# Doubling triangular inverses: all products of a step in front of its copies

## The chip, the cores and the metric

The kernel runs on one core of one Trainium2 chip. The metric is the device time of one execution in microseconds (us), median of several runs. TensorE (PE) multiplies and writes to PSUM; VectorE (DVE) and ScalarE (ACT) read PSUM and work in SBUF; GpSimd (POOL) works in SBUF; SyncE (SP) issues most DMA. Each engine takes its instructions in one fixed order and waits on semaphores for what others make.

## The reference

Two layers on 256 tokens of width 1024. Each layer adds half a SwiGLU feed-forward block (inner width 2816), a mixer, and half a feed-forward block again; all matrices are float32. The mixer projects the normed input with `w_in`, gives one part to a bidirectional gated DeltaNet (4 heads of 128) and one to a Hyena group (512 channels), and maps both back with `w_out`:

```python
o_dn = _deltanet_group(q, k, v, z, beta_logit, alpha, ...)
o_hy = _hyena_group(hy_in, hy_conv[i], ...)
x = x + jnp.concatenate([o_dn, o_hy], axis=-1) @ w_out[i]
```

The DeltaNet works in chunks and needs, for each head, chunk and direction, the solution of a unit triangular system:

```python
a_mat = jnp.where(strict, jnp.einsum("bhnid,bhnjd->bhnij", kb, k) * decay, 0.0)
a_mat = a_mat + jnp.eye(c, dtype=q.dtype)
sol = lax.linalg.triangular_solve(a_mat, rhs, left_side=True, lower=True, unit_diagonal=True)
```

The output of each head is normed (`_rmsnorm(o, norm_w)`) and multiplied by `silu(z)`; the Hyena output is normed too.

## The kernel before

The kernel uses chunks of 128 tokens, so there are 2 chunks x 2 directions x 4 heads = 16 systems of 128x128. They stand in four quads `q_` = 0 to 3 of four heads each: quads 0 and 1 are the forward direction (first and second chunk), quads 2 and 3 the backward one (`S[:, 8 + h]` and `S[:, 12 + h]`). Two tiles hold the inverses as they grow: `S`, and `ST`, its transpose. Blocks of 16 are made first, and the stage "lvl" joins them to 32 (tiles `pz`, `pp`). The stage "quad" doubles twice, n = 32 and n = 64: for each pair of blocks a, b one product `pzq` (off-diagonal block of the system by `ST`), a copy to SBUF by ScalarE (`zq`), and then a product each for `S` (copied with a sign by VectorE) and `ST` (copied by ScalarE), both in one PSUM tile `ppq`. At n = 64 quads 0 and 1 need only `S`, quads 2 and 3 only `ST`.

Products of n = 32 occupy a 32x32 part of TensorE's array, those of n = 64 a 64x64 part, all others the whole 128x128.

Around it stand, by stage: "lc1" (long convolution of Hyena: `py`, `ze`, `zo`), "z" (projection `pw` of the gate z), "hn" (products `py2`, the Hyena norm: sums `st`, `nv`, GpSimd's power `pw__3775`, `dg`, `rbp`, `rb`), "hw" (`yn`, split in a high and a low half `yp` by ScalarE and VectorE, then the products `acc` of the Hyena half of `w_out`), "solve" (eight groups `ph` with VectorE and ScalarE steps `uf`, `ub`, `rho`, `gv` between), "o" (`po`; squares `osq`, sums `oss`, GpSimd's powers `pw__3991` and `pw__4013`, `on`), "ow" (transposes `pot`, gate `og`, split `yp`, and the DeltaNet half of `acc`). The names with numbers are those of layer 1; layer 2 has the same with others.

The program is written in this sequence, but it isn't executed in it: a scheduler of the framework simulates the engines and orders the instructions of each by readiness and by priorities of the stages (table `PRM`, `stage(...)`). So a change of dependences in "quad" lays out everything around it anew. VectorE also makes the low halves of the weights (`wl`), after ScalarE's high halves (`wh`); GpSimd makes the low halves of weights for the next block (`early`). All matrix products but `pot` go through one helper and show as line 118.

PSUM is taken by tags with two buffers each: `pzq`, `ph` and `po` have tag a, `pot` tag b, `py` tag c, `ppq` tag d, and the accumulators `acc` take c and d.

Of the kernel before, what the change touches and what calls it, by code (L numbers as in the profile page):

```python
# [10 lines left out]
F32 = mybir.dt.float32  # L11
# [78 lines left out]
def trunk_kernel(ctx: ExitStack, tc: tile.TileContext, xt, ffn, wba, win, wout, par, fpar, fwo, fnorm, con, feat, wnd, out):  # L90
# [7 lines left out]
    mx = ctx.enter_context(tc.tile_pool(name="mx", bufs=1))  # L98
# [15 lines left out]
    def psum(tag, name, shape=(128, 4, 128)):  # L114
        return ps.tile(list(shape), F32, tag=tag, name=name, bufs=2)

    def mm(o, l, r, start=True, stop=True, **kw):
        PE.matmul(o, lhsT=l, rhs=r, start=start, stop=stop, **kw)  # L118
# [72 lines left out]
    def rsqrt(v, n, tag):  # L191

        if tag[:2] in PRM["powr"]:
            y = sm.tile([128, n], F32, tag=tag, name="pw_")
            G.tensor_tensor(out=y, in0=v, in1=mhalf[:, 0:n], op=ALU.pow)
            return y
        sh = sm.tile([128, n], U32, tag=f"ns{n}", name="ns")
        V.tensor_scalar(out=sh, in0=v.bitcast(U32), scalar1=1, scalar2=None, op0=ALU.logical_shift_right)
        y0 = sm.tile([128, n], I32, tag=f"ny{n}", name="ny")
        V.tensor_scalar(out=y0, in0=sh.bitcast(I32), scalar1=-1.0, scalar2=float(0x5f3759df), op0=ALU.mult, op1=ALU.add)  # L200
        y = y0.bitcast(F32)
        for i in range(3):
            a = sm.tile([128, n], F32, tag=f"na{n}", name="na")
            V.tensor_tensor(out=a, in0=y, in1=y, op=ALU.mult)
            b = sm.tile([128, n], F32, tag=f"nb{n}", name="nb")
            V.scalar_tensor_tensor(out=b, in0=a, scalar=-0.5, in1=v, op0=ALU.mult, op1=ALU.mult)
            c = sm.tile([128, n], F32, tag=tag if i == 2 else f"nc{n}", name="nc_")
            V.scalar_tensor_tensor(out=c, in0=b, scalar=1.5, in1=y, op0=ALU.add, op1=ALU.mult)
            y = c
        return y  # L210
# [296 lines left out]
    def mixer(l, ys, norm, ab, wcols):  # L507
# [202 lines left out]
        for a in range(2):  # L710
            for hp in (slice(0, 2), slice(2, 4)):
                p = psum("a", "gram", (128, 2, 2, 128))
                for i in range(2):
                    h = hp.start + i
                    mm(p[:, i], kq[:, h, 0, a * 128:(a + 1) * 128], kq[:, h, 0])
                for i in range(2):
                    h = hp.start + i
# [18 lines left out]
        for a in range(2):  # L736
            both, one = ((Ef0, Eb[0, 0]), (Eb1, Ef[1, 1]))[a]
            for hp in (slice(0, 2), slice(2, 4)):
                p = psum("d", "kqp", (128, 2, 2, 128))
                for i in range(2):  # L740
                    h = hp.start + i
# [30 lines left out]
        for r in range(6, -1, -1):  # L772
            n = 7 - r
# [21 lines left out]
        S = mx.tile([128, 16, 128], F32, tag="S", name="S", bufs=1)  # L795
# [22 lines left out]
        for q_ in range(4):  # L818
            qs = slice(4 * q_, 4 * q_ + 4)
            p = psum("a", "stp")  # L820
# [10 lines left out]
        for q_ in range(4):  # L831
# [8 lines left out]
            pp = psum("d", "pp", (128, 2, 4, 4, 16))  # L840
# [38 lines left out]
        stage("quad")  # L879

        for n in (32, 64):
            for q_ in range(4):
                qs = slice(4 * q_, 4 * q_ + 4)
                pz = psum("a", "pzq", (128, 4, n))
                pp = psum("d", "ppq", (128, 4, n))
                zq = mx.tile([128, 4, n], F32, tag=f"zq{n}", name="zq", bufs=(2 if n == 32 else 1))
                for o in range(0, 128, 2 * n):
                    a, b = slice(o, o + n), slice(o + n, o + 2 * n)
                    for h in range(4):
                        mm(pz[b, h], XX[q_][a, h, b], ST[a, 4 * q_ + h, a])  # L890
                    A.activation(out=zq[b], in_=pz[b], func=AF.Copy)
                    if n == 32 or q_ < 2:
                        for h in range(4):
                            mm(pp[a, h], zq[b, h], S[b, 4 * q_ + h, b])
                        V.tensor_scalar(out=S[a, qs, b], in0=pp[a], scalar1=-1.0, scalar2=None, op0=ALU.mult)
                    if n == 32 or q_ >= 2:
                        for h in range(4):
                            mm(pp[b, h], S[b, 4 * q_ + h, b], zq[b, h])
                        A.activation(out=ST[b, qs, a], in_=pp[b], func=AF.Copy, scale=-1.0)

        stage("lc1")
# [19 lines left out]
        for i in range(4):  # L921
            c = slice(i * 128, (i + 1) * 128)
# [24 lines left out]
        def heads(tag, lh, r):  # L947
            p = psum(tag, "ph")
            for h in range(4):
                mm(p[:, h], lh(h), r[:, h])  # L950
            return p
# [12 lines left out]
        p = heads("a", lambda h: ST[:, 12 + h], gv1)  # L964
        ub[1] = d2("ub1")
        A.activation(out=ub[1], in_=p, func=AF.Copy)
        p = heads("a", lambda h: Mf[:, h], uf[0])
        V.tensor_tensor(out=rho[1], in0=rho[1], in1=p, op=ALU.subtract)
        p = heads("a", lambda h: Mb[:, h], ub[1])
# [3 lines left out]
        p = heads("a", lambda h: ST[:, 8 + h], gv0)  # L973
# [6 lines left out]
        for i in range(2):  # L980
# [10 lines left out]
            f = rsqrt(ss, 4, f"of{i}")  # L991
# [34 lines left out]
    for l in range(DEPTH):  # L1026
        P = par_s[:, l]
        ab = []
        side = chain(filters(l, ab), repeat(0, PRM["ej"]), ahead([win[l, i] for i in range(8)], PRM["ea"]))
        ys, norm = ffn_block(l, 0, ys, norm, P[:, C_NM:C_NM + 8], side)  # L1030
        ys, norm = mixer(l, ys, norm, ab, P[:, C_N2:C_N2 + 8])
        nxt = par_s[:, l + 1, C_N1:C_N1 + 8] if l + 1 < DEPTH else None
        ws = [ffn[l + 1, 0, j, i] for j in range(2) for i in range(2)] if l + 1 < DEPTH else []
        ys, norm = ffn_block(l, 1, ys, norm, nxt, chain(repeat(0, PRM["fj"]), ahead(ws, PRM["fa"])))
# [114 lines left out]
```

## Time and profile before

| What | Value |
|---|---|
| median of 3 runs | 1250.51 us (1249.68 to 1251.75) |
| profiled execution | 1253.56 us, span 1251.8 us |
| mean granted clock of TensorE | 0.982 |
| busy share of the span | PE 97%, DVE 70%, ACT 47%, POOL 25% |
| chain that ended last | PE 71%, DVE 13%, DMA 8%, ACT 3%, issue 3%, POOL 1% |

The span is the time from the first to the last instruction; the execution's own time also holds what lies around it. The chain follows the work back from the last instruction, at each step to what released it. The granted clock tells how fast the chip let TensorE run: 1.0 is full speed, 0.5 half. Line numbers below are those of the kernel before; in the changed one lines behind the stage are five higher.

### The profile page before, as it was taken

The numbers are of one execution on the slowest core, as the hardware profiler recorded it, in microseconds if no ns is written. First come the engines' busy times: TensorE is split into PE (matmuls) and PEld (weight loads), VectorE is DVE, ScalarE is ACT, GpSimd is POOL, SyncE is SP. The second block draws the span as 40 slices with busy tenths as digits, with TensorE's granted clock in tenths as the row PEclk, the third lists the DMA queues.
The fourth block names the chain that finished last, engine by engine and source line by source line (L and its number), as shares of the span: only waits on it lengthen the run. The fifth ranks groups of instructions, "written<-read, shape, count | busy, mean of one in ns | idle before, by whom it ended". The sixth has DMA issues, their size and how long they took to land.

```text
span 1251.8 us, 20519 instructions
## 1 busy us (share of the span) xinstructions
PE 1210.9 (97%) x7908; PEld 1063.9 (85%) x7908; DVE 875.5 (70%) x1483; ACT 588.8 (47%) x1058; POOL 306.8 (25%) x254
## 2 busy tenths in 40 slices
PE   6999989999999999999999999999999999999997
PEld 5888878978779899998888888888887898999996
DVE  6866677659954666667777767776597656766665
ACT  5544455362323445555554445553432334555553
POOL 5122233211221521113221214430202314111111
PEclk9999999999998899999999999999999988999998
DMA  8555667123222445556645556650231414455551
GB/s 292 172 168 192 195 204 228 31 68 101 69 74 96 135 135 188 190 188 204 210 127 188 181 168 210 222 169 16 77 111 51 136 60 143 156 186 188 193 186 53
DMA packets 53913, 186.36 MB, mean 149 GB/s; under 512 B 6157, under 2 KB 7088, under 8 KB 53816
## 3 DMA queue, kind: packets, MB, share of 16 engines
q1 hardware_dynamic: 50156, 179.01, 43.9%
q10 hardware_dynamic: 3660, 6.05, 1.6%
q8 instruction: 62, 1.02, 0.3%
q14 instruction: 35, 0.29, 0.1%
HBM read 183.98 MB, written 1.05 MB: 148 GB/s over the span
## 4 chain that ended last, share of the span: by engine, by line
PE 71%; DVE 13%; DMA 8%; ACT 3%; issue 3%; POOL 1%; DVEq 0%; SPq 0%; ACTq 0%
PE acc L118 18%; PE g L118 15%; PE u L118 14%; PE pw L118 10%; DMA raw<-in_win 6%; DVE wl L182 4%; DMA raw<-in_ffn 2%; PE py L118 1%; ACT wh L179 1%; PE pe L118 1%; PE pp L118 1%; PE ppq L118 1%; PE ph L118 1%; PE st L118 1%; DVE vs L552 1%
## 5 line engine op out<-in xcount | busy, mean ns | idle before, releaser
L182 DVE TENSOR_TENSOR wl<-raw,wh 128x1024 fp32r<-128x1024 f32 (+1 forms) x270 | 341.4, 1267 | 84.8 <-ACT wh L179 81.2
L179 ACT ACTIVATE wh<-raw 128x1024 fp32r<-128x1024 f32 (+1 forms) x270 | 282.1, 1048 | 121.0 <-PE acc L118 76.0
L118 PE MATMUL acc<-hp,wh 128*128 128x256 f32 x1408 | 265.9, 282 | 0.0
L118 PE MATMUL g<-yp,wh 128*128 128x512 f32 x656 | 245.0, 407 | 8.6 <-DVE yp L157 8.6
L118 PE MATMUL u<-yp,wh 128*128 128x512 f32 x656 | 236.0, 395 | 0.5 <-DVE ub L333 0.3
L118 PEld LDWEIGHTS acc<-hp,wh 128*128 128x128 f32 x1408 | 227.4, 190 | 3.6 <-issue 0.8
L368 POOL TENSOR_TENSOR sr<-gb,rb 128x256 f32<-128x256 f32 x88 | 110.4, 1254 | 450.7 <-ACT gb L366 450.7
L118 PE MATMUL acc<-hp,wl 128*128 128x256 f32 x704 | 194.3, 284 | 8.7 <-DVE wl L182 8.7
L118 PE MATMUL u<-yp,wl 128*128 128x256 f32 x656 | 168.9, 278 | 2.9 <-DVE wl L182 2.9
L118 PE MATMUL g<-yp,wl 128*128 128x256 f32 x656 | 171.7, 282 | 0.0
L118 PEld LDWEIGHTS g<-yp,wh 128*128 128x128 f32 x656 | 124.2, 189 | 40.6 <-DVE yp L157 9.7
L118 PE MATMUL pw<-y,raw 128*128 128x256 f32 x640 | 148.6, 381 | 0.0
L118 PEld LDWEIGHTS acc<-hp,wl 128*128 128x128 f32 x704 | 133.3, 190 | 13.0 <-DVE wl L182 11.1
L118 PEld LDWEIGHTS u<-yp,wh 128*128 128x128 f32 x656 | 123.2, 188 | 22.6 <-PE g L118 0.6
L118 PEld LDWEIGHTS pw<-y,raw 128*128 128x128 f32 x640 | 120.1, 190 | 25.9 <-issue 11.5
L118 PEld LDWEIGHTS u<-yp,wl 128*128 128x128 f32 x656 | 122.9, 188 | 11.3 <-DVE wl L182 4.3
L118 PEld LDWEIGHTS g<-yp,wl 128*128 128x128 f32 x656 | 124.6, 191 | 5.2 <-issue 1.4
L182 POOL TENSOR_TENSOR early<-raw,early 128x512 fp32r<-128x512 f32 (+1 forms) x44 | 75.5, 1729 | 93.9 <-ACT early L179 93.9
L332 ACT ACTIVATE gb<-g 128x256 f32<-128x256 f32 x88 | 33.4, 380 | 120.7 <-PE g L118 117.7
L153 DVE TENSOR_TENSOR hp<-ub,hp 128x256 fp32r<-128x256 f32 x88 | 56.8, 645 | 26.8 <-ACT hp L152 26.6
L333 DVE TENSOR_TENSOR gb<-g,gb 128x256 f32<-128x256 f32 x88 | 37.0, 420 | 44.3 <-ACT gb L332 44.3
L333 DVE TENSOR_TENSOR ub<-u,ub 128x256 f32<-128x256 f32 x88 | 37.0, 420 | 38.4 <-ACT ub L332 38.4
(436 smaller groups left out, 1669.8 us busy)
## 6 DMA issues: line engine op xcount, KB each, us to landing
raw<-in_ffn SPq DMA_DIRECT2D x264, 512.0 KB, 3.9
raw<-in_win SPq DMA_DIRECT2D x56, 512.0 KB, 4.5
raw<-in_wout SPq DMA_DIRECT2D x16, 512.0 KB, 3.9
w<-in_wnd ACTq DMA_DIRECT2D x16, 256.0 KB, 4.4
wo<-in_fwo ACTq DMA_DIRECT2D x8, 130.0 KB
X<-in_xt SPq DMA_DIRECT2D x4, 256.0 KB, 7.5
con_s<-in_con SPq DMA_DIRECT2D x1, 544.0 KB, 9.2
out<-X SPq DMA_DIRECT2D x2, 256.0 KB, 2.5
```

The source lines that it names most:

```text
L118: PE.matmul(o, lhsT=l, rhs=r, start=start, stop=stop, **kw)
L153: eng.tensor_tensor(out=lo, in0=src, in1=hi.bitcast(F32), op=ALU.subtract)
L179: op = A.activation(out=h, in_=raw[:, c], func=AF.Copy)
L182: eng.tensor_tensor(out=l_, in0=raw[:, c], in1=h.bitcast(F32), op=ALU.subtract)
L332: A.activation(out=t, in_=o[:, 1], func=AF.Copy)
L333: V.tensor_tensor(out=t, in0=o[:, 0], in1=t, op=ALU.add)
L368: G.tensor_tensor(out=sr, in0=sg, in1=norm.rb, op=ALU.mult)
L552: i = V.scalar_tensor_tensor(out=dst[:, lo:hi], in0=raw[:, lo + s_:hi + s_], scalar=P[:, w0 + j:w0 + j + 1], in1=dst[:, lo:hi], op0=ALU.mu ...
```

## The change

Only the stage "quad" is rewritten. The quads come in the sequence 0, 3, 1, 2. Within a quad the `pzq` products of all pairs stand first, then their copies `zq`, then all products for `S` and `ST`, alternating per head, and then all copies. The SBUF tiles `zq` of both levels share two buffers (named `zqd`); before, n = 32 had two and n = 64 one. Since VectorE's and ScalarE's copies of a quad read the same PSUM tile `ppq` and now stand one behind the other, they wait for each other (`S` of the first pair, `ST` of the first, `S` of the second, ...).

```diff
@@ -879,23 +879,28 @@
         stage("quad")
 
         for n in (32, 64):
-            for q_ in range(4):
+            for q_ in (0, 3, 1, 2):
                 qs = slice(4 * q_, 4 * q_ + 4)
                 pz = psum("a", "pzq", (128, 4, n))
                 pp = psum("d", "ppq", (128, 4, n))
-                zq = mx.tile([128, 4, n], F32, tag=f"zq{n}", name="zq", bufs=(2 if n == 32 else 1))
-                for o in range(0, 128, 2 * n):
-                    a, b = slice(o, o + n), slice(o + n, o + 2 * n)
+                zq = mx.tile([128, 256], F32, tag="zq", name="zqd", bufs=2)[:, 0:4 * n].rearrange("p (h c) -> p h c", h=4)
+                halves = [(slice(o, o + n), slice(o + n, o + 2 * n)) for o in range(0, 128, 2 * n)]
+                to_s, to_st = n == 32 or q_ < 2, n == 32 or q_ >= 2
+                for a, b in halves:
                     for h in range(4):
                         mm(pz[b, h], XX[q_][a, h, b], ST[a, 4 * q_ + h, a])
+                for a, b in halves:
                     A.activation(out=zq[b], in_=pz[b], func=AF.Copy)
-                    if n == 32 or q_ < 2:
-                        for h in range(4):
+                for a, b in halves:
+                    for h in range(4):
+                        if to_s:
                             mm(pp[a, h], zq[b, h], S[b, 4 * q_ + h, b])
+                        if to_st:
+                            mm(pp[b, h], S[b, 4 * q_ + h, b], zq[b, h])
+                for a, b in halves:
+                    if to_s:
                         V.tensor_scalar(out=S[a, qs, b], in0=pp[a], scalar1=-1.0, scalar2=None, op0=ALU.mult)
-                    if n == 32 or q_ >= 2:
-                        for h in range(4):
-                            mm(pp[b, h], S[b, 4 * q_ + h, b], zq[b, h])
+                    if to_st:
                         A.activation(out=ST[b, qs, a], in_=pp[b], func=AF.Copy, scale=-1.0)
 
         stage("lc1")
```

The scheduler's order of the engines shows where this goes. TensorE, layer 1, the first 32-wide quads between the products of the z projection (`pw`) and of the convolution (`zo`, `ze`); before:

```order
L118 MATMUL pw<-y_2422,raw 128x256 x2
L118 MATMUL ppq<-S,zq 32x32 x4
L118 MATMUL pzq<-ST,ex 32x32 x3
L118 MATMUL ppq<-S,zq 32x32 x4
L118 MATMUL pzq<-ST,ex 32x32 x5
L118 MATMUL zo<-zt,con_s 128x512
L118 MATMUL pw<-y_2417,raw 128x256 x4
L118 MATMUL pw<-y_2422,raw 128x256 x4
L118 MATMUL ppq<-zq,S 32x32 x8
L118 MATMUL ze<-zt,con_s 128x512
L118 MATMUL pw<-y_2417,raw 128x256 x2
```

and after, from the end of the first group of sixteen `ppq` products on:

```order
L118 MATMUL ppq<-zqd,S 32x32
L118 MATMUL ppq<-S,zqd 32x32
L118 MATMUL ppq<-zqd,S 32x32
L118 MATMUL pzq<-ST,ex 32x32 x8
L118 MATMUL pzq<-ST,xf 32x32 x8
L118 MATMUL zo<-zt,con_s 128x512
L118 MATMUL pw<-y_2417,raw 128x256 x3
L118 MATMUL pw<-y_2422,raw 128x256 x4
L118 MATMUL pw<-y_2417,raw 128x256 x2
L118 MATMUL ppq<-S,zqd 32x32
L118 MATMUL ppq<-zqd,S 32x32
```

The products for S and ST of several quads, and the next `pzq`, are now in one run instead of four groups with `pw` between.

TensorE, layer 1, from the Hyena half of `acc` to the DeltaNet half, before:

```order
L118 MATMUL acc<-yp,wl 128x256
L118 MATMUL acc<-yp,wh 128x256 x2
L118 MATMUL acc<-yp,wl 128x256
L118 MATMUL acc<-yp,wh 128x256
L997 MATMUL pot<-con_s,on 128x128 x8
L118 MATMUL acc<-yp,wh 128x256
L118 MATMUL acc<-yp,wl 128x256
```

and after, where the end of `po` and the beginning of the Hyena half of `acc` meet:

```order
L118 MATMUL po<-uf_3964,ef_2510 128x128
L118 MATMUL po<-ub_3943,eb_2499 128x128
L118 MATMUL po<-uf_3936,ef_2498 128x128
L118 MATMUL po<-uf_3964,ef_2510 128x128
L118 MATMUL po<-ub_3943,eb_2499 128x128
L118 MATMUL rbp<-dg,con_s 128x128 x2
L1002 MATMUL pot<-con_s,on 128x128 x2
L118 MATMUL acc<-yp,wh 128x256
L118 MATMUL acc<-yp,wl 128x256
```

Before, `ph` and `po` lay between the first `acc` products, and the eight `pot` between the two halves; now all `po` stand in front of the first `acc`, `rbp` and two `pot` between them, and six `pot` between the halves.

VectorE, layer 1, around the head norm (`oss`, `on`), before:

```order
L182 TENSOR_TENSOR wl<-raw,wh 128x1024 x2
L989 TENSOR_REDUCE oss_3988<-osq 128x4
L990 SCALAR_TENSOR_TENSOR oss_3988<-oss_3988,ssq 128x4
L955 TENSOR_TENSOR on<-po,pw__3991 128x512
L989 TENSOR_REDUCE oss_4010<-osq 128x4
L990 SCALAR_TENSOR_TENSOR oss_4010<-oss_4010,ssq 128x4
L182 TENSOR_TENSOR wl<-raw,wh 128x1024
L955 TENSOR_TENSOR on<-po,pw__4013 128x512
L999 SCALAR_TENSOR_TENSOR og<-pot,par_s,zs 128x256 x2
L182 TENSOR_TENSOR wl<-raw,wh 128x1024
L999 SCALAR_TENSOR_TENSOR og<-pot,par_s,zs 128x256 x2
```

and after:

```order
L994 TENSOR_REDUCE oss_3988<-osq 128x4
L252 TENSOR_SCALAR nv<-st 128x2
L995 SCALAR_TENSOR_TENSOR oss_3988<-oss_3988,ssq 128x4
L256 TENSOR_SCALAR dg<-con_s,pw__3775 128x128 x2
L960 TENSOR_TENSOR on<-po,pw__3991 128x512
L994 TENSOR_REDUCE oss_4010<-osq 128x4
L942 SCALAR_TENSOR_TENSOR yn<-x_3614,par_s,rb 128x256
L942 SCALAR_TENSOR_TENSOR yn<-x_3631,par_s,rb 128x256
L942 SCALAR_TENSOR_TENSOR yn<-x_3648,par_s,rb 128x256
L942 SCALAR_TENSOR_TENSOR yn<-x_3665,par_s,rb 128x256
L995 SCALAR_TENSOR_TENSOR oss_4010<-oss_4010,ssq 128x4
L153 TENSOR_TENSOR yp<-yn,yp 128x256 x4
```

`yn` and `yp` of the Hyena norm stood ahead of the solves' last steps; they now stand behind the first `on` and the second `oss` reduction.

## Rows read from the trace of the kernel before

**Rows 1.** Windows, z projection of layer 1: window; busy (count) per engine; PEclk; DMA.

```profile
360.00:380.00 20.00, 20.00 (x162) 16.41 (x160) 16.69 (x23) 7.50 (x17) 8.63 (x5) 1.00 0.49 157
```

**Rows 2.** Windows cut to the three stretches of low clock, layer 1.

```profile
347.60:351.00 3.40, 3.40 (x9) 2.07 (x9) 0.75 (x2) 0.00 (x0) 0.00 (x0) 0.50 0.00 0
388.50:395.40 6.90, 6.90 (x38) 6.44 (x38) 2.48 (x7) 2.05 (x6) 0.71 (x1) 0.51 0.00 0
419.30:426.10 6.80, 6.07 (x26) 5.78 (x27) 6.80 (x7) 3.04 (x8) 6.73 (x4) 0.50 0.57 172
```

**Rows 3.** TensorE's waits, 340 to 432 us: total, times, longest.

```profile
PE pot L997 <- DVE on L955: 1.0, 1, 1.0
PE acc L118 <- ACT yp L152: 0.7, 1, 0.7
PE ppq L118 <- ACT zq L891: 0.5, 1, 0.5
PE pot L997 <- DVE og L999: 0.5, 1, 0.5
PE acc L118 <- DVE yp L153: 0.5, 1, 0.5
```

**Rows 4.** TensorE's timeline, z projection: start, duration, engine, line, out<-in, tile, shape, count.

```profile
352.40 1.03 PE L118 MATMUL pw<-y,raw 128*128 128x256 f32 x4
353.36 0.34 PE L118 MATMUL ppq<-S,zq 32*32 32x32 f32 x5
...
360.28 1.03 PE L118 MATMUL pw<-y,raw 128*128 128x256 f32 x4
361.14 1.02 PE L118 MATMUL zo<-zt,con_s 128*128 128x512 f32 x2
...
376.63 1.13 PE L118 MATMUL pw<-y,raw 128*128 128x256 f32 x4
```

**Rows 5.** TensorE's timeline, solves and first `acc`.

```profile
389.53 2.07 PE L118 MATMUL ph<-rho,S 128*128 128x128 f32 x8
...
396.15 0.37 PE L118 MATMUL acc<-yp,wh 128*128 128x256 f32 x1
...
396.47 0.28 PE L118 MATMUL acc<-yp,wh 128*128 128x256 f32 x1
...
397.19 1.05 PE L118 MATMUL ph<-ub,mb 128*128 128x128 f32 x8
```

**Rows 6.** VectorE's timeline, from the first `yn` to the last `yp`; waits in brackets.

```profile
394.25 1.67 DVE L937 SCALAR_TENSOR_TENSOR yn<-x,par_s,rb 128x256 f32<-128x256 f32 x4 [1.92 <-ACT rb L261]
395.84 1.43 DVE L153 TENSOR_TENSOR yp<-yn,yp 128x256 fp32r<-128x256 f32 x4
...
402.18 1.22 DVE L182 TENSOR_TENSOR wl<-raw,wh 128x1024 fp32r<-128x1024 f32 x1 [0.64 <-ACT wh L179]
...
409.34 0.69 DVE L989 TENSOR_REDUCE oss<-osq 128x4 f32<-128x512 f32 x1 [1.96 <-ACT osq L987]
...
411.35 0.69 DVE L955 TENSOR_TENSOR on<-po,pw__3991 128x512 f32<-128x512 f32 x1 [1.12 <-POOL pw__3991 L195]
...
420.25 6.07 DVE L153 TENSOR_TENSOR yp<-og,yp 128x256 fp32r<-128x256 f32 x4
```

**Rows 7.** ScalarE's timeline, same place.

```profile
394.77 0.81 ACT L152 ACTIVATE yp<-yn 128x256 fp32r<-128x256 f32 x2 [0.55 <-DVE yn L937]
...
408.71 0.60 ACT L987 ACTIVATE osq<-po 128x512 f32<-128x512 f32 x1 [2.59 <-PE po L118]
```

**Rows 8.** GpSimd's timeline, same place.

```profile
388.84 0.71 POOL L195 TENSOR_TENSOR pw__3775<-nv,mhalf 128x2 f32<-128x2 f32 x1 [1.83 <-DVE nv L252]
410.31 1.01 POOL L195 TENSOR_TENSOR pw__3991<-oss,mhalf 128x4 f32<-128x4 f32 x1 [20.75 <-DVE oss L990]
...
414.46 1.93 POOL L195 TENSOR_TENSOR pw__4013<-oss,mhalf 128x4 f32<-128x4 f32 x1
419.29 6.74 POOL L182 TENSOR_TENSOR early<-raw,early 128x1024 fp32r<-128x1024 f32 x4 [2.90 <-ACT early L179]
```

## The prediction

> **What bounds the kernel now.** I read the engine shares on the profile's page first, then the windows with the granted clock, then TensorE's waits, then its timeline through one mixer and at last VectorE, ScalarE and GpSimd beside it. On the page TensorE is busy 97% of the span and holds 71% of the chain that ended last: what counts is TensorE's own time, and every idle or slowed microsecond on it is one of the total. While the mixer of layer 1 runs the z projection it has no gap at all [rows 1]. What it loses is of two kinds. The clock: in three stretches of a layer its granted clock is 0.50, the lower of its two levels (1.2 instead of 2.4 GHz), while it is busy [rows 2]: about 3.4 us behind the 16-wide level of the inverses (call it A), 6.9 us over the last 64-wide products and the first solves (B), 6.8 us over the output projection's second half (C). Layer 2 has the same three, 614.4 us later. Before A come 32x32 products and products of 64 columns, before B 64x64 products with waits between, before C transposes with waits between: each time TensorE had done little for some microseconds. And the waits: five in layer 1, 3.2 us together [rows 3], and the same five in layer 2, which I take at layer 1's length.
>
> **The change part by part.** The instructions are the same in kind and number; the program's scheduler lays them out anew in both layers. All terms are per layer unless I say otherwise.
>
> *Fewer changes of tile size.* From the first doubling product to the last transpose of the heads, TensorE's order changes between 32x32, 64x64 and 128x128 tiles 31 times before and 14 times after, counted off the two orders. The price is read in the timeline [rows 4]: four records of `pw` take 0.86 us from their start to the next group's (360.28 to 361.14) with no change around them; 0.96 where a 32x32 group follows (352.40 to 353.36); and behind such a group their own duration is 1.13 against 1.03. So 0.10 us on the way in and 0.10 on the way out. 17 x 0.10 = 1.7 us off; bounds 0 (if the alternating products each pay something) and 17 x 0.11 = 1.9. I take 1.7, since it comes from rows of just these groups.
>
> *Fewer changes between solve and output projection.* Before, `ph` and `po` stand inside the Hyena half of `acc`, and the first `acc` behind one takes 0.37 us against 0.28 for one behind another [rows 5]. There are seven such returns, after the change two: 5 x 0.09 = 0.4 us off.
>
> *Waits that go.* The 64-wide product that waits 0.5 us for `zq` [rows 3] gets other work in front of it. The transposes `pot` no longer wait for the second `on` (1.0 us [rows 3]): both `on` are made before the Hyena half of `acc` starts, and 96 `acc` products lie between. Together 1.5 us off. The other three waits at the tail (for `og`, for ScalarE's `yp`, for VectorE's `yp`) stay: the chain behind the last `pot` is the same.
>
> *A wait that comes.* With all `po` in front of the first `acc`, TensorE has after the last `po` only two `rbp` products and two transposes until the first `yp`. Two things now stand ahead of `yn` in VectorE's queue: the first `on`, which waits for GpSimd's `pw__3991`, and the second `oss` reduction. The second `st` pair lies seven `po` products before the end, at most 7 x 0.26 = 1.8 us (a `ph` product is 1.05 / 4 [rows 5]), say 1.6. Behind it: `nv`, the first `oss`, GpSimd's 0.71 and 1.01 one after the other [rows 8] and the hand-overs, some 2.2 us, so `on` starts about 0.6 us after the last `po`. Then `on` 0.69, the reduction 0.69, one `yn` 0.42 (1.67 / 4), one `yp` of ScalarE 0.40 (0.81 / 2) and 0.2 of hand-overs [rows 6, 7]: the first `acc` is 3.0 us after the last `po`. About 0.8 of it is `rbp` and `pot`, so TensorE idles 2.2 us. Its ninth product needs VectorE's first `yp`, which stands behind all four `yn`; that is another 0.3. Sum 2.5 us on. Bounds: 1.9 if GpSimd's powers are out of the way in time (then only ScalarE's `osq` 0.60, reduction, `yn` and `yp` are in the chain, less the 0.8, with the 0.3 and hand-overs), 4.4 if VectorE's `yp` also wait for `pw__4013` (1.93 [rows 8]).
>
> *Copies in a row.* ScalarE's copy to ST now waits for VectorE's copy to S of the same PSUM tile, and the second half's S copy for the first half's ST copy. Queued behind on ScalarE are copies and activations of the projections. I cost it at 0: TensorE has `pw` products beside it, and ScalarE is busy only 7.50 of the 20 us there [rows 1]. If that cover fails, one `wl` of VectorE in front of an S copy holds ScalarE for up to 1.2 us [rows 6]: bound 0 to 1.2. The solves come earlier, among `pw` and `py2`; two `wl` stand among their VectorE steps, so the same bound, and 0, holds for them. At A four of the 32-wide groups become one, which takes 0.6 us of fill away from the 16-wide level: 0 to 0.6, I take 0.
>
> *The clock.* The mixture that B follows (64x64 products, waits, `st`) is taken apart: these products now stand between `pw`, and the solves too. B's 6.9 us at half speed are 3.4 us lost, and I let them go. `ph` of eight records shows the size: 2.07 us in B, 1.05 behind it [rows 5]. But the change makes two thin places of its own: a run of forty 32x32 and four 64x64 products in the middle of the projection, and the idle place before the first `acc`. Of the three stretches before, A lasted half as long as B and C. I take one new stretch as long as A in each layer (1.7 us lost), A and C as they are. Bounds: no new stretch (0), and one as long as C at the first `acc` (3.4).
>
> *The sum.* -1.7 - 0.4 - 1.5 + 2.5 - 3.4 + 1.7 = -2.8 us per layer, -5.6 in all: the profiled execution's 1253.56 (its span is 1251.8, the rest lies around it) becomes 1248.0. That execution is 3.05 us above the median of the runs, 1250.51; from there the same sum gives 1244.9, which I predict.
>
> A rule that speaks against it: VectorE's four `yp` behind `yn` take 1.43 us where GpSimd is idle, and 6.07 us where GpSimd converts early weights for 6.74 us [rows 6, 8]; in the changed order `pw__4013` comes beside these `yp`. The Trainium skill (SBUF — State Buffer, Who interferes with whom) says that a VectorE instruction with two SBUF inputs contends with a GpSimd instruction that reads SBUF, and that whoever issues first holds the other off for its whole length. The trace agrees with its 6.07. By that rule the `yp` could lose up to one `pw__` each layer (1.0 to 1.9 us); by the order VectorE issues its first `yp` while GpSimd still waits for the `oss` that precedes it, and loses little.
>
> **The rivals.**
> 1. No new slow stretch: the quads, cut only by a few `pw`, and the gap before `acc` don't lower the clock. For it: 32x32 groups between `pw` at 360 to 380 us ran at 1.00 [rows 1]. Against: those came 16 records at a time, the new run has five times as many. Then 2 x 1.7 more: 1241.5; if A goes as well, 1238.1. Chance 0.17.
> 2. The half clock only moves: B goes, and a stretch of its length comes at the quads or at the first `acc`. The sum loses 2 x 1.7: 1248.3; with 1 to 2 us for copies in a row and the 16-wide level, 1249 to 1251. For it: C follows a stretch with about 2.6 us of waits [rows 3], which is as thin as my 2.5. Against: C has waits in four places. Chance 0.23.
> 3. Slower: the VectorE queue before `yn`. If `pw__3991` and `pw__4013` are as slow as 1.93, `on`, `yn` and `yp` all come late; the wait is 4.4 instead of 2.5, and the place is then emptier than the one before C, so that it costs a stretch of 6.8 (3.4 us) beside the new one of A's length at the quads. Per layer 1.9 + 3.4 more than the forecast, +2.5 net: +5.0 in all, 1255.5. It decides from the length of the gap at which the clock falls for so long: then a layer stands at -2.8 + 3.4 = +0.6, the whole at 1251.7, and every microsecond that the gap grows in both layers adds two. For it: the first `on` waits 1.1 us for `pw__3991` before as well [rows 6], and after the change nothing fills TensorE there. Against: the powers are short where nothing contends [rows 8]. Chance 0.24.
>
> The forecast has the rest, 0.36, with 1241.5 to 1248 as its own range.
>
> **How the numbers follow.** A measurement of this kernel can't tell less than 0.2%, 2.5 us, from no change: 1248.0 to 1253.0 counts as the same. The forecast and rival 1 are faster: 0.53. Rival 2 lies in the band, with a little of the forecast's upper edge and of rival 3's lower: 0.24. Slower 0.23. For the range I cut the case without A at its lower end and the worst of rival 3: 1238 to 1256.5.
>
> **What would show it.** Right: the granted clock 1.0 over the 64-wide products and the solves; no idle time at `pot` for `on`; an idle time of 2 to 3 us before the first `acc` of each mixer, released by ScalarE's `yp`; four `pw` records behind 32x32 groups still 0.1 longer, but fewer such places. Wrong: half clock in the quads or over the first `acc` products for as long as B; a wait of TensorE for S or ST copies or for `ph`'s inputs of more than 1 us; or gaps in `pw` because ScalarE hangs behind VectorE's copies.

## The result and the profile after

The changed kernel takes 1238.45 us (four runs, 1236.98 to 1239.72) against 1250.1 for the kernel before: a ratio of 0.9899 (95% interval 0.9882 to 0.9916), 11.65 us or 1% less. The forecast was 5.6 us less. The sign was right and the time lies in the range, near its lower end, but the gain is twice the forecast, and that the time lies in the range is luck (below).

The profiled execution took 1238.01 us. First its clock, from the view of the cores (span and mean granted clock):

```profile
core 0: 1236.2 us, clock 0.989
```

One minus the mean clock, times the span, is the time that half speed takes away: (1 - 0.982) x 1251.8 = 22.5 us before and (1 - 0.989) x 1236.2 = 13.6 now, some 9 us less. It is more than what half speed costs, since it counts idle time too: in both kernels some 10 us at the end of the program are at half clock (from 1241.87 before and 1225.97 now), with TensorE busy for 1.2 of them. The windows of the changed kernel, cut to what answers to [rows 1, 2] (window; busy per engine; granted clock; DMA):

```profile
342.30:376.40 34.10, 34.10 (x386) 27.38 (x385) 21.28 (x38) 12.40 (x32) 8.55 (x5) 1.00 0.27 87
376.40:392.50 16.10, 16.10 (x138) 15.90 (x138) 7.19 (x15) 5.05 (x10) 2.69 (x4) 1.00 0.35 114
396.54:399.95 3.41, 3.41 (x18) 3.41 (x18) 1.41 (x4) 0.00 (x0) 1.59 (x1) 0.50 0.00 0
413.60:420.43 6.83, 4.32 (x20) 4.32 (x21) 3.46 (x4) 0.45 (x1) 2.17 (x1) 0.50 0.62 233
1017.76:1024.59 6.83, 3.78 (x17) 3.78 (x18) 4.00 (x5) 0.05 (x1) 2.58 (x1) 0.50 0.63 230
```

The quads, the z projection, the solves and `po` now run at 1.00 from beginning to end: A and B are both gone, in layer 2 as well. What is left at half clock in the mixers is 3.41 us over the first `acc` products of layer 1, and 6.83 us over the DeltaNet half of `acc` (C) in each layer. TensorE is busy for only 4.32 and 3.78 us of these 6.83: C begins in a wait. Counted by TensorE's busy time alone, both mixers together had 32.8 us at half clock before and have 11.5 now; half of the difference, 10.6 us, is what the clock gave.

TensorE's waits in layer 1 (total, times, longest), for [rows 3]:

```profile
PE acc L118 <- DVE yp L153: 3.5, 1, 3.5
PE acc L118 <- ACT yp L152: 2.1, 2, 1.2
PE pot L1002 <- DVE on L960: 0.7, 1, 0.7
PE pot L1002 <- DVE og L1004: 0.5, 1, 0.5
```

`pot` for the second `on` and `ppq` for `zq` have gone, as forecast (the `on` of the second row is the first one). But the sum is 6.8 us instead of 3.2, and 3.5 of it is one wait of `acc` for VectorE's `yp`. Layer 2 has the same, 6.8 us for 3.5 before.

The quads on TensorE, beside [rows 4] (start, duration, line, names, tile, shape, count):

```profile
352.58 4.05 PE L118 MATMUL pw<-y,raw 128*128 128x256 f32 x18
356.56 0.21 PE L118 MATMUL ppq<-S,zqd 32*32 32x32 f32 x1
356.56 0.21 PE L118 MATMUL ppq<-zqd,S 32*32 32x32 f32 x1
...
357.75 0.68 PE L118 MATMUL pzq<-ST,xf 64*64 64x64 f32 x8
```

Two records of 32x32 start at the same time (a product leaves two records). From 356.56 to the first 64x64 product at 357.75 lie 64 `ppq` and 16 `pzq` records: 1.19 us, 0.015 each. In the kernel before, sixteen stood alone:

```profile
358.70 0.69 PE L118 MATMUL ppq<-zq,S 32*32 32x32 f32 x16
359.32 1.12 PE L118 MATMUL ze<-zt,con_s 128*128 128x512 f32 x2
```

These take 0.62 us up to the next start, of which 0.10 are the change of tile size: 0.033 each. That was in no term of the sum.

The gap before the first `acc`:

```profile
392.49 0.61 PE L118 MATMUL rbp<-dg,con_s 128*128 128x128 f32 x4
393.82 0.41 PE L1002 MATMUL pot<-con_s,on 128*128 128x128 f32 x2 [0.72 <-DVE on L960]
395.16 0.39 PE L118 MATMUL acc<-yp,wh 128*128 128x256 f32 x1 [0.93 <-ACT yp L152]
```

From the last `po` to the first `acc` it is about 2.7 us, of which TensorE idles 1.65 (forecast 3.0 and 2.2). And the tail, VectorE, GpSimd and TensorE:

```profile
408.76 1.89 DVE L1004 SCALAR_TENSOR_TENSOR og<-pot,par_s,zs 128x256 f32<-128x256 f32 x4 [0.67 <-PE pot L1002]
411.02 2.56 DVE L182 TENSOR_TENSOR wl<-raw,wh 128x1024 fp32r<-128x1024 f32 x1 [0.36 <-ACT wh L179]
413.50 3.56 DVE L153 TENSOR_TENSOR yp<-og,yp 128x256 fp32r<-128x256 f32 x4
```

```profile
410.12 2.38 POOL L182 TENSOR_TENSOR early<-raw,early 128x1024 fp32r<-128x1024 f32 x1 [11.99 <-ACT early L179]
413.24 2.54 POOL L182 TENSOR_TENSOR early<-raw,early 128x1024 fp32r<-128x1024 f32 x1 [0.74 <-ACT early L179]
```

```profile
411.35 0.39 PE L118 MATMUL acc<-yp,wh 128*128 128x256 f32 x1 [1.22 <-ACT yp L152]
...
416.11 0.80 PE L118 MATMUL acc<-yp,wh 128*128 128x256 f32 x2 [3.54 <-DVE yp L153]
```

VectorE's `wl` at 411.02 takes 2.56 us and not 1.22 [rows 6], because GpSimd has begun a conversion at 410.12 (`hold_early` below shows it); the first `yp` behind it meets the next conversion, begun at 413.24, and TensorE stands for 3.54 us. Before the change this `wl` stood between the two pairs of `og`; now it stands behind all four and in front of `yp`.

### The profile page after: what moved, and what is told of

It reads as the page before. It is cut to its first block, busy times and chain, and to the rows that moved or that the text cites. A ratio compares the mean times of both kernels' runs of the same rounds, so it can differ in the third digit from the quotient of the medians.

```text
span 1236.2 us, 20507 instructions
## 1 busy us (share of the span) xinstructions
PE 1191.8 (96%) x7908; PEld 1050.0 (85%) x7908; DVE 867.8 (70%) x1483; ACT 588.1 (48%) x1058; POOL 304.8 (25%) x254
## 4 chain that ended last, share of the span: by engine, by line
PE 71%; DVE 13%; DMA 8%; issue 3%; ACT 3%; POOL 1%; DVEq 0%; SPq 0%; ACTq 0%
PE acc L118 19%; PE u L118 15%; PE g L118 15%; PE pw L118 11%; DMA raw<-in_win 6%; DVE wl L182 4%; DMA raw<-in_ffn 2%; PE pe L118 1%; ACT wh L179 1%; PE pp L118 1%; PE py L118 1%; PE st L118 1%; DVE vs L552 1%; PE ph L118 1%; ACT early L179 1%
## 5 line engine op out<-in xcount | busy, mean ns | idle before, releaser
L368 POOL TENSOR_TENSOR sr<-gb,rb 128x256 f32<-128x256 f32 x88 | 110.2, 1253 | 451.4 <-ACT gb L366 451.4
L118 PEld LDWEIGHTS pw<-y,raw 128*128 128x128 f32 x640 | 120.4, 191 | 24.7 <-issue 10.5
L118 PEld LDWEIGHTS u<-yp,wl 128*128 128x128 f32 x656 | 123.9, 189 | 10.6 <-DVE wl L182 3.7
```

The lines of the kernel that those rows point to most:

```text
L368: G.tensor_tensor(out=sr, in0=sg, in1=norm.rb, op=ALU.mult)
```

## The experiments

Each kernel was timed beside the kernel before on the same chip. That kernel's median was 1251.67 us beside `sides_grouped`, `four_in_turn`, `alternate_only` and `order_only`, 1250.46 beside `body_only`, `own_buffers`, `hold_early` and `hold_early_yp`, 1249.92 beside the two `repeat` kernels and `yn_first`, and 1251.92 beside `early_on_dve`. A ratio is to that median, with its 95% interval.

**Side by side or not.** `sides_grouped` is the changed kernel with the products of a pair grouped by side:

```diff
                     for h in range(4):
                         if to_s:
                             mm(pp[a, h], zq[b, h], S[b, 4 * q_ + h, b])
+                    for h in range(4):
                         if to_st:
```

> The changed kernel, but within a pair of blocks the four products for S stand first and then the four for ST, instead of in turn per head; the order of everything else on TensorE is the same piece by piece. Theory P (products on different parts of the array, issued in turn, run side by side): the 32-wide products take about 0.6 us per 16 records again, as before the change, so a layer loses up to 3.3 us of the 3.3 that they gained, less what still overlaps where one group of four meets the next: 1241 to 1245 us, with the ppq rows in the trace longer and nothing else changed. Rival R (the gain comes from fewer changes of tile size, less half clock and fewer waits, and the closer ppq records are no time): the same time as the changed kernel, 1238.5, within 2 us.

Measured 1239.68 us (ratio 0.9896, 0.9876 to 0.9917), 1.2 more than the changed kernel and within what its runs spread: by the total alone P's 1241 to 1245 is missed and R's figure met. The trace tells more. Its order on TensorE is otherwise the same piece by piece. Added over the timeline (from the start of each record to the start of the next), the `ppq` records fill 4.61 us of TensorE's time per layer against 3.46 in turn: 1.15 us, a third of what theory P said. The reason is in its trace:

```profile
348.14 0.34 PE L118 MATMUL ppq<-S,zqd 32*32 32x32 f32 x5
348.30 0.21 PE L118 MATMUL ppq<-zqd,S 32*32 32x32 f32 x1
348.32 0.19 PE L118 MATMUL ppq<-S,zqd 32*32 32x32 f32 x1
```

The group for ST starts before the group for S has ended, so even groups of four on neighbouring parts overlap. In the kernel before, a copy stands between the two groups in the program, and on TensorE other products do (`ze` above), so they could not.

`four_in_turn` exchanges the two loops, so that four neighbours lie on four parts:

```diff
-                for a, b in halves:
-                    for h in range(4):
+                for h in range(4):
+                    for a, b in halves:
```

> The changed kernel with the products of both pairs of blocks in turn at n = 32, so that four successive products lie on four different parts of the array instead of two; the order of instructions is otherwise the same. Theory P: at least as fast; if four parts overlap as two do, the 128 records of a layer fall from about 1.7 us to 0.9, 1.6 us in both layers: 1237 us, at worst no change. Rival R: no change, 1238.5.

Measured 1237.51 us (ratio 0.9885, 0.9861 to 0.991). `ppq` fills 3.03 us per layer, 0.43 less than in turn by two. The direction is P's, the size a half of what it gave at best, and the total can't tell P's 1237 from R's 1238.5.

To make the cost large enough for the total, `repeat_in_turn` and `repeat_apart` issue each product four times:

```diff
-                    for h in range(4):
+                    for h in [h for _ in range(4) for h in range(4)]:
```

> The changed kernel with each of the products for S and ST issued four times into the same place (the repeats write the same values), in turn between the part of the array for S and that for ST. Per layer 384 more records of 32x32 and 96 of 64x64. Theory P (adjacent products on different parts of the array overlap): the changed kernel's trace shows 64 records in turn in about 0.7 us, so 384 cost about 4 us, and the 64-wide ones (one side only) 96 x 0.067 = 6.4: 10.4 per layer, 1259 us, half clock aside. Rival R (each costs the same, the close records are no time): 384 x 0.039 = 15 and 6.4, 1281 us.

> As repeat_in_turn, but the sixteen products for S of a pair in one run and then the sixteen for ST, so that neighbours lie on the same part of the array. Theory P: 384 x 0.039 = 15 us and 6.4 per layer: 1281 us, some 20 us more than repeat_in_turn. Rival R: the same as repeat_in_turn.

Measured 1275.97 (ratio 1.0192, 1.0167 to 1.0216) and 1295.74 (1.0364, 1.0349 to 1.038): 19.8 us apart, where P said some 20 and R none. Both are 15 to 17 us dearer than P's figures, and their mean clock is lower, 0.975 and 0.970, with half clock in the quads where the changed kernel has none. The first group of layer 1 in each (windows from its first record to the next other product; 128 `ppq` and 32 `pzq` records):

```profile
348.15:350.81 2.66, 2.66 (x162) 2.62 (x161) 1.25 (x3) 0.86 (x3) 0.00 (x0) 1.00 0.58 203
```

```profile
348.10:353.45 5.35, 5.35 (x162) 5.29 (x161) 1.25 (x3) 1.01 (x4) 0.00 (x0) 0.79 0.32 101
```

The 2.66 us are at full clock; the 5.35 have a mean clock of 0.79, so 4.2 at full clock. With the changed kernel's and `sides_grouped`'s 1.14 and 1.44 us for the same group without repeats (350.48 to 351.62 and 348.14 to 349.58), 96 more records cost 1.52 us in turn (0.016 each) and 2.8 apart (0.029). So neighbours on different parts cost about half. The difference in mean clock is worth some 7 us, (1 - 0.970) x 1292.8 less (1 - 0.975) x 1276.4; the products are the other 13 of the 19.8, and that the sum comes so near to P's figure is luck. R's "the same" is out by far.

**Which part of the change.** `alternate_only` is the kernel before with the products in turn per pair, in front of that pair's copies:

```diff
+                    for h in range(4):
+                        if n == 32 or q_ < 2:
+                            mm(pp[a, h], zq[b, h], S[b, 4 * q_ + h, b])
+                        if n == 32 or q_ >= 2:
+                            mm(pp[b, h], S[b, 4 * q_ + h, b], zq[b, h])
```

> The kernel before with one edit: within a pair of blocks the products for S and ST stand in turn per head in front of the two copies; order of the quads, copies per pair and buffers as before. The scheduler's order then has 27 changes of tile size per layer (before 31, after 14). Theory P: most of the gain of the small products comes with this alone: 6 us less than before, 1244, and more if the clock keeps up. Rival R: 0.8 us less by the four changes of tile size that are saved, so 1249, unless the layout changes the half clock.

Measured 1243.31 us (ratio 0.9937, 0.9916 to 0.9957), as P said; the profiled execution is the slowest of the five, 1248.26. `ppq` fills 4.48 us per layer (7.72 and 7.29 in the two layers before, about 1 us of it half clock). But its layout also has the long tail wait:

```profile
PE acc L118 <- DVE yp L153: 3.5, 1, 3.5
PE acc L118 <- ACT yp L152: 1.6, 1, 1.6
```

`order_only` has nothing but the new sequence of the quads:

```diff
-            for q_ in range(4):
+            for q_ in (0, 3, 1, 2):
```

> The kernel before with one edit: the quads come as 0, 3, 1, 2. TensorE's order then has 37 changes of tile size per layer. Theory P: no side-by-side products, so 1250 +- 3 from the layout alone. Rival R (solves ready earlier and the layout make the gain): the solves can start earlier, 1240 to 1246.

Measured 1237.29 us (ratio 0.9899, 0.9856 to 0.9941): the whole gain, without the products in turn and with 37 changes of tile size. `ppq` and `pzq` fill 6.44 and 4.53 us per layer (changed kernel 3.46 and 3.58). What is saved is the clock:

```profile
core 0: 1235.1 us, clock 0.995
```

(1 - 0.995) x 1235.1 = 6.2 us, 16.3 less than before, for 14.4 measured. It differs from run to run: this execution took 1236.85 us, the others had a mean clock of 0.992, 0.993 and 0.989, and the one at 0.989 took 1245.08. A's and B's places and what is left at half clock, and the waits of layer 1:

```profile
347.60:351.00 3.40, 3.40 (x29) 2.13 (x28) 1.57 (x4) 0.98 (x2) 0.00 (x0) 1.00 0.21 36
385.00:395.00 10.00, 9.62 (x86) 9.27 (x85) 7.16 (x17) 3.34 (x8) 1.07 (x2) 1.00 0.00 0
...
413.10:416.50 3.40, 3.03 (x13) 2.37 (x14) 2.86 (x3) 2.17 (x5) 2.92 (x2) 0.50 0.63 187
```

```profile
PE pot L997 <- DVE on L955: 1.4, 1, 1.4
PE pot L997 <- DVE og L999: 1.1, 1, 1.1
PE acc L118 <- DVE yp L153: 0.7, 2, 0.4
```

That is outside P's 1247 to 1253, and beyond R's 1240 to 1246; R's cause (solves ready earlier) is seen in part: the first `ph` starts at 385.2 and not at 389.5. But it takes no wait away, since TensorE's waits in the mixer of layer 1 add up to 3.2 us, as before. Neither theory had the clock as a source of its own; whether the earlier solves are what keeps it up at B's place is not shown.

`body_only` is the changed kernel with the old sequence:

```diff
-            for q_ in (0, 3, 1, 2):
+            for q_ in range(4):
```

> The changed kernel with the quads in their old sequence 0, 1, 2, 3. TensorE's order has 11 changes of tile size per layer (14 in the changed kernel), and all po stand in front of acc as in the changed kernel. Theory K (the total follows the half-clocked time, the idle time and the small products, and the body of the change decides the products): products as in the changed kernel, the tail wait too: 1236 to 1241. Rival: the sequence of the quads is the source of the gain: 1245 to 1250.

Measured 1236.13 us (ratio 0.9874, 0.9844 to 0.9904): the whole gain again, with 11 changes of tile size, `ppq` 3.59 us and some 6.8 us of idle time per mixer, as K said. So each of the two parts alone gives what both give together, by different ways: the sequence nearly all by the clock, the body by the products and the clock, less the tail wait. They don't add.

`own_buffers` takes back the shared buffers:

```diff
-                zq = mx.tile([128, 256], F32, tag="zq", name="zqd", bufs=2)[:, 0:4 * n].rearrange("p (h c) -> p h c", h=4)
+                zq = mx.tile([128, 4, n], F32, tag=f"zq{n}", name="zq", bufs=(2 if n == 32 else 1))
```

> The changed kernel with separate zq buffers again (two for n = 32, one for n = 64). One buffer at n = 64 makes the next zq wait for the last product of the quad before. Theory K: the shared buffers matter by at most 1 us per layer: 1238.5 to 1241. Rival (the buffers are what lets the quads run ahead): 1243 or more.

Measured 1237.83 us (ratio 0.9886, 0.9862 to 0.991): the buffers are worth nothing that shows here.

**The tail wait.** `hold_early` puts ScalarE's early conversions behind its last `yp` of the heads, and so GpSimd's too:

```diff
+            if early is not None and after_[0] is not None:
+                behind(op, after_[0])
```

(`after_[0]` is ScalarE's last `yp` of the heads while these weights are loaded, `behind` an order on one engine.)

> The changed kernel with one edit behind the quads: ScalarE's conversions of the early weights stand behind its last yp of the heads, so that GpSimd's low halves of them start only then. In the profile of the changed kernel VectorE's wl (2.56 us beside a GpSimd conversion, 1.22 alone) and the first of its yp come late there, and TensorE waits 3.5 us per layer for that yp. Theory C (that wait is contention of VectorE with GpSimd, and the half clock behind it comes from the wait): the wait falls by 2 to 3 us per layer and the half clock over the DeltaNet half of acc goes or gets shorter: 1228 to 1234 us. Rival D (the wait is the order on VectorE, wl in front of yp): 2.4 us less in all, 1236.

Measured 1234.26 us (ratio 0.9866, 0.9839 to 0.9893), just above C's 1228 to 1234 and below D's 1236. The interval holds both, and the changed kernel's 0.9899 lies close by, so the traces have to decide. VectorE:

```profile
407.70 1.22 DVE L187 TENSOR_TENSOR wl<-raw,wh 128x1024 fp32r<-128x1024 f32 x1
408.84 0.42 DVE L156 TENSOR_TENSOR yp<-og,yp 128x256 fp32r<-128x256 f32 x1
```

`wl` stands in the same place, in front of the first `yp`, and takes 1.22 us again; the wait for VectorE's `yp` is 0.5 instead of 3.5. So the new order by itself does not make the wait; GpSimd beside `wl` and `yp` does. (The edit frees ScalarE as well: its `wh` and `yp` no longer stand behind an `early` conversion, and TensorE's wait for ScalarE's `yp` at the tail is gone.) Neither mixer has any half clock in this profile, but it isn't saved. It comes in the feed-forward block behind the mixer, after a new wait for `ub` (TensorE's timeline, and the window: length, busy per engine, clock):

```profile
440.39 0.69 PE L118 MATMUL u<-yp,wh 128*128 128x512 f32 x1 [2.83 <-DVE ub L338]
```

```profile
440.48:443.89 3.41, 3.41 (x12) 2.92 (x13) 2.67 (x8) 1.30 (x4) 0.75 (x2) 0.50 0.50 156
```

Layer 2 has the same from 1044.64, and the first feed-forward block 6.83 us from 160.58. Over the whole span TensorE is busy at half clock for 13.3 us here and for 12.7 in the changed kernel. So C was right on the wait; on the clock it holds for the mixers alone.

`hold_early_yp` also puts the third head's `wl` behind the last `yp`:

```diff
+        behind(late, split[1])
```

(`late` is that `wl`, `split[1]` VectorE's last `yp`.)

> As hold_early, and VectorE's wl for the third head's weights stands behind its last yp. Theory C: another 1.2 us per layer less than hold_early, unless the wait behind has another cause: 1226 to 1232 us. Rival D: the whole gain comes here, 1231, and hold_early shows little.

Measured 1231.19 us (ratio 0.9843, 0.9819 to 0.9867), in C's range and at D's 1231. VectorE and GpSimd there:

```profile
408.27 0.42 DVE L157 TENSOR_TENSOR yp<-og,yp 128x256 fp32r<-128x256 f32 x1
...
409.00 1.09 DVE L157 TENSOR_TENSOR yp<-og,yp 128x256 fp32r<-128x256 f32 x3
410.00 1.22 DVE L188 TENSOR_TENSOR wl<-raw,wh 128x1024 fp32r<-128x1024 f32 x1
```

```profile
410.57 11.47 POOL L188 TENSOR_TENSOR early<-raw,early 128x1024 fp32r<-128x1024 f32 x6 [12.85 <-ACT early L183]
```

The `yp` now take 0.36 us each and the conversions begin behind them. The wait for VectorE's `yp`, 1.0 us in both layers with `hold_early`, is gone. The total is 3 us lower, but the two intervals overlap; both edits together, 7 us below the changed kernel, are clear of it. They have a price: GpSimd converts six halves in a row until 422, when the next block has begun, and TensorE waits in that block (whole execution):

```profile
PE u L118 <- DVE ub L339: 6.1, 3, 2.9
...
PE acc L118 <- ACT yp L156: 1.9, 2, 0.9
```

`ub` had 0.3 us in the changed kernel. Its two long waits end at 440.43 and 1042.49, in layer 1 18 us behind the last conversion, so what leads from one to the other isn't shown.

`yn_first` adds to `hold_early_yp` the order of `four_in_turn`, and puts the second `oss` reduction behind the `yn`:

```diff
+            if i == 1:
+                behind(red, yn_last)
```

> The version hold_early_yp with the products of all four parts in turn (four_in_turn) and the second oss reduction behind the yn on VectorE. Theory K (time follows TensorE's idle time, half clock and the products): the wait of the first acc for yp falls from 0.9 to 0.3 us per layer, the products by 0.4: 2 us less than hold_early_yp, 1229. Rival: the gap in front of acc has other causes (rb, the first on), 1231.

Measured 1231.72 us (ratio 0.9853, 0.9838 to 0.9867): the rival's figure, and K's 1229 is missed. Nothing is decided by it: the first `acc` waits for ScalarE's `yp` 0.7 us in both layers together instead of 1.9, but VectorE's `yp` then come 0.9 late, and more of the run is at half clock (mean clock 0.992 against 0.993); the sum is as before.

`early_on_dve` is `hold_early_yp` with the first two early low halves on VectorE:

```diff
-            early.append(load_w(src, eng=G, early=SLOT[t]))
+            early.append(load_w(src, eng=V if after_[0] is not None and i < 2 else G, early=SLOT[t]))
```

> The version hold_early_yp, with the low halves of the first two early weights of the second feed-forward block made by VectorE instead of GpSimd. In hold_early_yp GpSimd works on six such halves until the next block has begun (11.5 us in a row), and TensorE waits 6.1 us for ub behind it and 1.1 for the first yp. Theory K (these waits are what the held conversions cost): both fall to under 1 us each in sum, 5 us less than hold_early_yp: 1226 us. Rival (VectorE, with 2.4 us more per layer, becomes late for X or wl instead): 1230 to 1233.

Measured 1226.7 us (ratio 0.9797, 0.9771 to 0.9824), the fastest of all, 25 us less than before and as K said to within a microsecond. The waits it was made for (whole execution):

```profile
PE g L118 <- DVE yp L161: 12.3, 5, 8.5
...
PE u L118 <- DVE ub L339: 0.3, 1, 0.3
```

`ub` is at 0.3 again, so its wait did come with the six conversions in a row on GpSimd. The wait for the first `yp` of a block didn't fall (12.3 us in all against 10.5 in `hold_early_yp`), so the second half of the reason given failed.

## Why the prediction was wrong in part

The sign was right, the size was not, and three terms of the sum failed. Per layer, the small products were put at -1.7 us and gave -4.1; the clock was put at -1.7 net and gave -3.4 in layer 1 and -5.1 in layer 2; and the waits at the tail, put at 0, came to +3.5. The first two fell short by some 5 us and the third took 3.5 of it back. That the time still lies in the range is luck. So is the 1238.1 of rival 1 with A gone, 0.4 us from the measured time: it had the clock better (A gone, though one new stretch came, in layer 1), and the forecast's figures for the other two terms.

**Fewer changes of tile size.** -1.7 us per layer were taken for 17 changes. Added over the timeline, the groups of small products take 12.6 us per layer before (1.0 of it lost to half clock, 0.5 the wait for `zq`) and 7.05 after: 4.1 less at full clock. The step failed by what it left out: it kept the cost per product, and the products now run side by side. The price of a change stands as read: `pw` x18 from 352.58 to 356.56 takes 3.98 us, 18 x 0.215 and 0.11. The gain was bounded at 0 to 1.9, since the alternating products "each pay something"; that they may gain was not asked. The Trainium skill (TensorEngine Tiling (Array Packing), Key Properties) says that different tiles can load weights and multiply in parallel. The trace agrees, with 0.015 us for 0.033 per record, and the two `repeat` runs show it in the total.

**The clock.** The forecast was 1.7 us per layer net (B goes, one new stretch as long as A comes). By the same reckoning, half the length of each stretch, it is 17.1 us in each layer before, 10.2 and 6.8 after: 3.4 and 5.1 us gained. A went as well, the run of small products in the projection didn't lower the clock, and of the new place before `acc` the profile shows it in one layer only. `order_only` shows that the clock by itself can be worth the whole gain.

**The waits that go** were right: `zq` and the second `on` no longer hold TensorE (0.5 and 1.0 us). **The wait that comes** before the first `acc` was 1.65 us and not 2.5: the first `acc` came 2.7 us after the last `po` instead of 3.0, more of it was `rbp` and `pot`, and the 0.3 of the ninth product didn't come. The powers didn't hold up VectorE's `yp` either (1.43 us for four, beside a `pw__4013` of 2.13), so rival 3 fell.

**The tail** is the step that failed outright. That its three waits stay, since "the chain behind the last `pot` is the same", was argued from the dependences. The order on VectorE had changed, just behind the piece of it shown with the change: `wl` had come between the `og` and `yp`. The wait grew by 3.0 us for VectorE's `yp` and by 0.5 for ScalarE's, in each layer, and C stayed with it. GpSimd's conversions were in the rows already, and the four `yp` of 6.07 us [rows 6] are those of the tail; but they were weighed against the `yp` behind `yn`. There they cost nothing, and at the tail 1.3 us on `wl` and 2.2 on the first `yp`. The rule on VectorE and GpSimd that the prediction took from the Trainium skill (SBUF — State Buffer, Who interferes with whom) was thus weighed at the wrong place. `hold_early` shows it: with `wl` in its new place and no GpSimd beside it, `wl` is 1.22 us again and the wait 0.5.

**Copies in a row** cost nothing, as taken: TensorE has no wait for S or ST copies.

The accounts of both profiled executions, in us over both layers: clock -10.6 (by busy time, so that waits at half clock are not counted twice), small products -8.1 (layer 1 taken twice), waits in the mixers +6.9 (3.6 and 3.3), returns from `ph` and `po` to `acc` -0.8 (as forecast, not tested). That is -12.6. The two mixers, from their first `pw` to the first `g` of the next block, took 209.6 and 210.0 us before and 204.0 and 202.1 after: 13.6 less, so 1.0 stays unexplained. The executions differ by 15.6 and the medians by 11.65; what differs outside the mixers isn't settled. What makes the clock fall at one thin place and not at another was not settled either; it is read from the profiles, not explained.

## What to carry to other kernels

Small products on different parts of the array cost about half here when they stood next to each other, so put what separates them (a copy, a wait) behind a whole group. Where a scheduler lays out the work, read the new order of every engine through the whole stage, also where the dependences have not changed: the dearest wait here came where one `wl` had changed its place and met GpSimd's conversions. And before adding up single terms, look at what half clock costs in the stage, by TensorE's busy time; a change that only moved work won all of its gain there, and two such changes didn't add.

## What was not expected of the hardware

The sequence of four quads alone was worth 14.4 us. A VectorE subtraction of 1.22 us took 2.56 when GpSimd had started on its own 0.9 us before it. And half clock moved with the wait: with the tail wait taken out, both mixers ran at full clock throughout (`hold_early`), and 3.41 us of half clock came in the block behind, after a wait of 2.83 us.
